# Low parts of the down-projection weights made by accumulating DMA transfers instead of by VectorE

## The chip, the cores and the metric

The kernel runs on one core of a Trainium2 chip. The core has TensorE (matrix products out of SBUF into PSUM), VectorE, ScalarE and GpSimd (POOL) for work by element, SyncE (SP), which here only issues transfers, and 16 DMA engines. Each engine takes its instructions in the order of its own queue and waits on semaphores for the others. The metric is the device time of one execution in microseconds. Times inside the kernel come from one profiled execution, counted from its first instruction.

## The reference

The reference is a trunk of two encoder layers on 256 positions of width 2048, in float32. Layer 0 mixes tokens by grouped-query attention, layer 1 by a dilated sliding-window attention. Each layer is followed by a gated MLP, which is where the change lies:

```python
D_MODEL = 2048
SEQ = 256
DEPTH = 2
D_FF = 5632
...
def conv_ffn(h, w_up, conv_w, conv_b, w_down):
    u = h @ w_up
    c = u.shape[-1]
    pad = CONV_WIDTH // 2
    u = lax.conv_general_dilated(u, conv_w[:, None, :].astype(u.dtype), window_strides=(1,),
                                 padding=((pad, pad),), dimension_numbers=('NWC', 'WIO', 'NWC'),
                                 feature_group_count=c) + conv_b
    gate, val = jnp.split(u, 2, axis=-1)
    return (jax.nn.silu(gate) * val) @ w_down
...
    for i in range(DEPTH):
        hn = rms_norm(h, mix_norm[i])
        ...
        h = h + conv_ffn(rms_norm(h, ffn_norm[i]), w_up[i], conv_w[i], conv_b[i], w_down[i])
    return rms_norm(h, final_norm)
```

The down-projection multiplies a 256 x 5632 matrix by the 5632 x 2048 weights `w_down`, once in each layer.

## The kernel before

**Precision.** TensorE takes its operands in a float32 format of lower precision (`F32R`). To come near float32, each matrix is split into a high part, which is the value rounded to that format, and a low part, which is the difference. A product is then made of three: high by high, high by low, low by high. For the weights, the high part `wh` is a copy made by ScalarE (line 139) and the low part `wl` a subtraction made by VectorE, `raw - wh` (line 140). For the activations the two parts lie in `ah` and `al` (in `xh` and `xl` elsewhere).

**The unit of work.** `feed` (line 114) handles 512 rows of a weight matrix by 512 columns. SP loads them as one transfer of 1 MB into a tile `raw` of 128 partitions by 4 x 512 values (line 118). The tile is worked on in two halves (`s` = 0 and 1), each of 128 x 1024 values: `wh`, `wl`, then 12 matmuls, which are three products for each of two groups of 128 rows of weights (`kt`) and two groups of 128 positions (`m`). The results add up in two PSUM tiles `accs`. After each half `step()` runs one stage of whatever work is pending, such as the transposition of earlier results.

**Buffers and order.** `raw` has three buffers (`NRAW`), `wh` and `wl` three each (`NHL`). The order of the instructions on each queue is made by a scheduler when the program is built, by priorities that follow the program's text. The work on `wh` and `wl` stands in `tc.high_priority(offset=AHEAD)` with `AHEAD` = 45, so it is placed as if it stood 45 instructions earlier, and it then waits for a free buffer rather than for its turn. A load of `raw` waits for the last reader of the buffer that it takes.

**The stages.** `ffn` (line 291) is called once for each layer. It does the MLP in two parts (`HALVES`), over 6 and then 5 groups of 512 inner columns: the up-projection by `feed_T` (line 90), with the convolution and the gate behind it, whose last product is made by GpSimd (`cv`, line 354), and then the down-projection of that part (lines 431 to 436). The down-projection goes over four column blocks `n`: blocks 0 and 1 together in `project2` (line 158), which leaves the last group of each to a late part, and blocks 2 and 3 by `project` (line 151), one after the other. A part has so 4 x 6 = 24 or 4 x 5 = 20 feeds, 88 in both layers. In the very last block the last feed is run with `by_m`: all matmuls of one group of positions first, so that its results can be finished early. In the second part of layer 1, the results of blocks 0 to 2 are multiplied by the final gain `fin` on GpSimd (line 399).

**Other users of the same code.** `feed` also serves the projections of both attentions, which the change leaves as they are.

Of the kernel before, what the change touches and what calls it, by code (L numbers as in the profile page):

```python
# [7 lines left out]
F32 = mybir.dt.float32  # L8
F32R = mybir.dt.float32r
AF = mybir.ActivationFunctionType  # L10
ALU = mybir.AluOpType
AX = mybir.AxisListType

P = 128
# [9 lines left out]
AHEAD = 45  # L24
# [4 lines left out]
def tile_encoder(ctx: ExitStack, tc: tile.TileContext, x, xT, w_a, w_ao, q_gain, k_gain, w_b, w_bo,  # L29
                 rel_bias, gains, w_up, conv, w_down, final_norm, rope, ident_c, onehot, out):  # L30
    nc = tc.nc
# [24 lines left out]
    def nm(s):  # L56
        uid[0] += 1
        return f"{s}_{uid[0]}"
# [15 lines left out]
    def start(gen):  # L74
        if next(gen, StopIteration) is not StopIteration:
            pending.append(gen)

    def step():
        while pending:
            if next(pending[0], StopIteration) is not StopIteration:  # L80
                return
            pending.pop(0)
        if spare and next(spare[0], StopIteration) is StopIteration:
            spare.pop(0)

    def drain(keep=0):
        while len(pending) > keep:
            step()
# [22 lines left out]
                                 start=False, stop=end and kt == 3)  # L111
            step()

    def feed(accs, lhs, kg, wap, first, last, by_m=False, pieces=1, mid=None):
        raw = spool.tile([P, 4, 512], F32, tag="raw", name=nm("raw"), bufs=NRAW)
        rawf, w = raw.rearrange("p a c -> p (a c)"), 2048 // pieces
        for i in range(pieces):
            nc.sync.dma_start(rawf[:, i * w:(i + 1) * w], wap[:, i * w:(i + 1) * w])
            if mid is not None:
                mid(i)  # L120
        def mms(order):
            for m, kt in order:
                (wh, wl), j = hls[kt // 2], kt % 2
                xh, xl = lhs[4 * kg + kt][:2]
                st, sp = first and kt == 0, last and kt == 3
                c = slice(m * P, (m + 1) * P)
                nc.tensor.matmul(accs[m], xh[:, c], wh[:, j, :], start=st, stop=False)  # L127
                nc.tensor.matmul(accs[m], xh[:, c], wl[:, j, :], start=False, stop=False)  # L128
                nc.tensor.matmul(accs[m], xl[:, c], wh[:, j, :], start=False, stop=sp)  # L129

        hls = []
        for s in range(2):
            wh = spool.tile([P, 2, 512], F32R, tag="wh", name=nm("wh"), bufs=NHL)
            wl = spool.tile([P, 2, 512], F32R, tag="wl", name=nm("wl"), bufs=NHL)
            r = raw[:, 2 * s:2 * s + 2, :]
            with tc.high_priority(offset=AHEAD):
                for i in range(max(pieces // 2, 1)):
                    c = slice(i, i + 1) if pieces == 4 else slice(0, 2)
                    nc.scalar.activation(wh[:, c], r[:, c], AF.Copy)  # L139
                    nc.vector.tensor_tensor(wl[:, c], r[:, c], wh[:, c].bitcast(F32), ALU.subtract)  # L140
            hls.append((wh, wl))
            if not by_m:
                mms([(m, kt) for kt in (2 * s, 2 * s + 1) for m in range(2)])
                step()
        if by_m:
            mms([(m, kt) for m in range(2) for kt in range(4)])

    def new_acc():
        return [accp.tile([P, 512], F32, tag="acc", name=nm("acc")) for _ in range(2)]

    def project(w, n, lhs, kgs, by_m=False):
        accs = new_acc()
        for i, kg in enumerate(kgs):
            end = i == len(kgs) - 1
            feed(accs, lhs, kg, w[n, kg], i == 0, end, by_m and end)
        return accs

    def project2(w, n0, n1, lhs, kgs, late, first_done, hook=None):
        a0, a1 = new_acc(), new_acc()
        early = len(kgs) - late  # L160
        for k, part in enumerate((range(early), range(early, len(kgs)))):
            if k == 1:
                drain()
            for accs, n in ((a0, n0), (a1, n1)):
                for i in part:
                    kg = kgs[i]
                    mid = hook and hook(n == n0, kg)
                    feed(accs, lhs, kg, w[n, kg], i == 0, i == len(kgs) - 1,
                         pieces=4 if hook and i < 2 else 2 if hook else 1, mid=mid)
                if k == 1 and n == n0:  # L170
                    first_done(a0)
        return a1
# [39 lines left out]
    def sumsq_cols(ss, n, junk):  # L212
        for m in range(2):
            nc.scalar.activation(junk(), h[:, m, n * 512:(n + 1) * 512], AF.Square,
                                 accum_out=ss[:, m, n:n + 1])
# [54 lines left out]
    def add_residual(accs, n):  # L270
        for m in range(2):
            hs = h[:, m, n * 512:(n + 1) * 512]
            nc.vector.tensor_tensor(hs, accs[m], hs, ALU.add)  # L273
# [17 lines left out]
    def ffn(l, hT, ss_in, g_next, last, side=None):  # L291
        with tc.tile_pool(name=nm("fpool"), bufs=1) as fp:
# [66 lines left out]
            kgs = list(range(4))  # L359
            for hf, (p0, p1) in enumerate(HALVES):  # L360
                slots = {}
# [29 lines left out]
                def done(accs, n):  # L391
                    if hf == 1 and last:
                        for m in range(2):
                            cols = slice(n * 512, (n + 1) * 512)
                            hs = h[:, m, cols]
                            nc.vector.tensor_tensor(hs, accs[m], hs, ALU.add)
                            if n < 3:
                                nc.scalar.activation(junk(), hs, AF.Square, accum_out=ss[:, m, n:n + 1])
                                nc.gpsimd.tensor_tensor(hs, hs, fin[:, cols], ALU.mult)
                            else:  # L400
                                nc.vector.scalar_tensor_tensor(junk(), hs, 1.0, hs, ALU.mult, ALU.mult,
                                                               accum_out=ss[:, m, n:n + 1])
                                finish(m)
                        if n == 2:
                            nc.vector.tensor_reduce(part, ss[:, :, :3], axis=AX.X, op=ALU.add)
                            nc.vector.tensor_scalar(part, part, 1.0 / D, EPS, op0=ALU.mult, op1=ALU.add)
                        return
                    add_residual(accs, n)
                    if hf == 1:
                        sumsq_cols(ss, n, junk)  # L410
                        start(late_transpose(hTn, n, g_next, fp, "tT"))

                def finish(m):
                    ms = small.tile([P, 1], F32, tag="ms", name=nm("ms"))
                    nc.vector.tensor_scalar(ms, ss[:, m, 3:4], 1.0 / D, part[:, m:m + 1],
                                            op0=ALU.mult, op1=ALU.add)
                    r = small.tile([P, 1], F32, tag="rstd", name=nm("rstd"))
                    nc.gpsimd.tensor_tensor(r, ms, nhalf[:, :1], ALU.pow)
                    for n in (3, 0, 1, 2):
                        hs = h[:, m, n * 512:(n + 1) * 512]  # L420
                        if n == 3:
                            nc.vector.scalar_tensor_tensor(hs, hs, r, fin[:, n * 512:(n + 1) * 512],
                                                           ALU.mult, ALU.mult)
                        elif n == 0 or m == 0:
                            nc.scalar.activation(hs, hs, AF.Copy, scale=r)
                        else:
                            nc.vector.tensor_scalar(hs, hs, r, None, op0=ALU.mult)
                        eng = nc.scalar if m == 1 and n % 2 == 0 else nc.sync
                        eng.dma_start(out.rearrange("(p m) c -> m p c", m=2)[m, :, n * 512:(n + 1) * 512], hs)

                np_ = p1 - p0
                drain(1)
                wd = w_down[l][:, p0:p1]
                done(project2(wd, 0, 1, slots, list(range(np_)), 1, lambda a: done(a, 0)), 1)
                for n in (2, 3):
                    done(project(wd, n, slots, list(range(np_)), last and hf == 1 and n == 3), n)
            assert not spare
        return hTn, ss

# [49 lines left out]
    def mixer_a():  # L489
        with tc.tile_pool(name="apool", bufs=1) as ap:  # L490
# [95 lines left out]
            def k_gen(accs):  # L586
# [9 lines left out]
                yield from heads_T_dve(kT, ro, ap, "sq")  # L596

            va = project2(w_a, 4, 5, hT, kgs, 1, lambda a: start(k_gen(a)), hook)
            v = evac_split(ap, va, rstd[0])

# [56 lines left out]
            for g in range(4):  # L657
                start(attend(g, project(w_a, g, hT, kgs)))
# [249 lines left out]
```

## Time and profile before

| | |
|---|---|
| time, median of 2 runs | 2312.73 us (2312.73 to 2312.74) |
| span of the profiled execution | 2312.0 us |
| mean granted TensorE clock | 0.999 |
| down-projection stages (first to last load of `w_down`) | 529 to 656, 883 to 991, 1823 to 1950, 2177 to 2283 us |
| loads of `w_down` | 88 of 1024 KB |
| data moved by DMA | 437.46 MB, mean 189 GB/s |

The page gives for each engine its busy time, its share of the span and its number of instructions; PEld are the weight loads of TensorE, which run beside its matmuls. In the rows of instructions, the first number of a timeline row is its start and the second its duration, in microseconds, and what stands in square brackets is the idle time ahead of it on its engine and who ended it. A row of waits gives the sum of the waits, their number and the longest. A row of a transfer ends with its size and the time from its issue to its landing. In a table of stretches, the last three columns are the granted TensorE clock, the busy share of the DMA engines and the rate that they moved. A matmul row lasts longer than the distance to the next one, since matmuls are pipelined: the distance is the cost.

### The profile page before, as it was taken

What the parts mean: (1) busy time and instruction counts of PE and PEld (TensorE: products, weight loads), DVE (VectorE), ACT (ScalarE), POOL (GpSimd) and SP (SyncE); (2) the same over time, 40 slices, a digit from 0 to 9 for tenths busy, and PEclk for the clock granted to TensorE, in tenths of its full rate; (3) what the DMA queues carried; (4) which work ended last, traced back from release to release, by engine and by line L of the source; (5) the groups of instructions that cost most, each with busy time, mean ns of one, the idle gap of its engine ahead of it and who ended that gap; (6) DMA issues with size and microseconds to landing.
All of it is one profiled execution on the core that took longest, in us unless ns stands there. A gap on an engine that the chain in (4) does not pass through costs nothing.

```text
span 2312.0 us, 30191 instructions
## 1 busy us (share of the span) xinstructions
PE 2292.1 (99%) x11641; PEld 1946.0 (84%) x11641; DVE 1613.9 (70%) x2321; ACT 1210.7 (52%) x1746; POOL 162.4 (7%) x127
## 2 busy tenths in 40 slices
PE   9999999999999999999999999999999999999998
PEld 7788788888888888888888888878888888888886
DVE  6877877676457776778776876586777754677755
ACT  6565565554345555455454554445555543555543
POOL 2210000010000010010000000000101100001010
PEclk9999999999999999999999999999999999999999
DMA  8444565665555555565555554556555555555554
GB/s 289 156 146 148 190 201 180 229 201 194 187 195 191 191 184 189 181 222 200 195 178 174 174 198 164 172 190 212 186 191 190 191 186 198 191 191 183 193 190 146
DMA packets 229024, 437.46 MB, mean 189 GB/s; under 512 B 10400, under 2 KB 193440, under 8 KB 201104
## 3 DMA queue, kind: packets, MB, share of 16 engines
q1 hardware_dynamic: 226976, 429.82, 55.2%
q0 software_dynamic: 1472, 5.15, 0.7%
q8 instruction: 91, 1.49, 0.3%
q10 hardware_dynamic: 432, 0.56, 0.1%
q14 instruction: 53, 0.43, 0.0%
HBM read 429.20 MB, written 6.29 MB: 188 GB/s over the span
## 4 chain that ended last, share of the span: by engine, by line
PE 89%; DVE 6%; DMA 2%; issue 1%; POOL 1%; ACT 1%; SPq 1%; POOLq 0%; DVEq 0%; ACTq 0%
PE acc L107 26%; PE acc L128 15%; PE acc L129 15%; PE acc L127 15%; PE acc L110 14%; DVE wl L140 2%; DVE tT L219 2%; DMA raw<-in_w_up_dram 2%; PE ps L190 1%; PE ps L194 1%; PE ps L193 0%; PE ps L192 0%; POOL t L576 0%; SPq L685 0%; DVE h L273 0%
## 5 line engine op out<-in xcount | busy, mean ns | idle before, releaser
L140 DVE TENSOR_TENSOR wl<-raw,wh 128x1024 fp32r<-128x1024 f32 (+1 forms) x456 | 552.6, 1214 | 333.1 <-ACT wh L139 329.5
L139 ACT ACTIVATE wh<-raw 128x1024 fp32r<-128x1024 f32 (+1 forms) x456 | 475.1, 1044 | 545.6 <-PE acc L129 494.5
L107 PE MATMUL acc<-xh,wh 128*128 128x512 f32 x2816 | 707.5, 393 | 3.1 <-ACT wh L102 3.0
L107 PEld LDWEIGHTS acc<-xh,wh 128*128 128x128 f32 x2816 | 507.1, 189 | 95.7 <-ACT wh L102 4.1
L103 DVE TENSOR_TENSOR wl<-raw,wh 128x1024 fp32r<-128x1024 f32 x352 | 431.7, 1228 | 202.1 <-ACT wh L102 191.7
L102 ACT ACTIVATE wh<-raw 128x1024 fp32r<-128x1024 f32 x352 | 372.1, 1058 | 311.1 <-PE acc L107 204.4
L110 PEld LDWEIGHTS acc<-xh,wl 128*128 128x128 f32 x2816 | 384.1, 190 | 27.5
L128 PE MATMUL acc<-wl,ah 128*128 128x512 f32 x1024 | 400.1, 391 | 2.5 <-DVE wl L140 2.2
L127 PE MATMUL acc<-wh,ah 128*128 128x512 f32 x1024 | 399.2, 390 | 0.0
L129 PE MATMUL acc<-wh,al 128*128 128x512 f32 x1024 | 398.8, 389 | 0.0
L110 PE MATMUL acc<-xh,wl 128*128 128x256 f32 x2816 | 392.6, 282 | 0.0
L127 PE MATMUL acc<-wh,xh 128*128 128x512 f32 x768 | 302.3, 394 | 0.9 <-ACT wh L139 0.9
L128 PE MATMUL acc<-wl,xh 128*128 128x512 f32 x768 | 300.3, 391 | 2.2 <-DVE wl L140 2.1
L129 PE MATMUL acc<-wh,xh 128*128 128x512 f32 x768 | 299.6, 390 | 0.0
L128 PEld LDWEIGHTS acc<-wl,ah 128*128 128x128 f32 x1024 | 192.3, 188 | 46.5 <-DVE wl L140 7.6
L127 PEld LDWEIGHTS acc<-wh,ah 128*128 128x128 f32 x1024 | 192.3, 188 | 39.7
L129 PEld LDWEIGHTS acc<-wh,al 128*128 128x128 f32 x1024 | 192.3, 188 | 39.4
L354 POOL TENSOR_TENSOR cv<-cg,cv 128x512 f32<-128x512 f32 x44 | 95.5, 2170 | 1165.4 <-DVE cv L346 975.4
L128 PEld LDWEIGHTS acc<-wl,xh 128*128 128x128 f32 x768 | 144.4, 188 | 32.6 <-DVE wl L140 5.3
L129 PEld LDWEIGHTS acc<-wh,xh 128*128 128x128 f32 x768 | 144.2, 188 | 29.9
L127 PEld LDWEIGHTS acc<-wh,xh 128*128 128x128 f32 x768 | 144.4, 188 | 29.4 <-ACT wh L139 1.7
L178 ACT ACTIVATE ah<-cv 128x256 fp32r<-128x256 f32 x88 | 32.0, 411 | 105.1 <-POOL cv L354 105.1
(152 smaller groups left out, 1374.8 us busy)
## 6 DMA issues: line engine op xcount, KB each, us to landing
raw<-in_w_up_dram SPq DMA_DIRECT2D x352, 512.0 KB
raw<-in_w_down_dram SPq DMA_DIRECT2D x88, 1024.0 KB
raw<-in_w_b_dram SPq DMA_DIRECT2D x72, 1024.0 KB
raw<-in_w_bo_dram SPq DMA_DIRECT2D x24, 1024.0 KB
raw<-in_w_a_dram SPq DMA_DIRECT2D x16, 1024.0 KB
raw<-in_w_ao_dram SPq DMA_DIRECT2D x16, 1024.0 KB
raw<-in_w_a_dram SPq DMA_DIRECT2D x16, 256.0 KB
raw<-in_w_a_dram SPq DMA_DIRECT2D x8, 512.0 KB
```

Source lines behind the costliest of these rows:

```text
L102: nc.scalar.activation(wh, rk, AF.Copy)
L103: nc.vector.tensor_tensor(wl, rk, wh.bitcast(F32), ALU.subtract)
L107: nc.tensor.matmul(acc[j], wh[:, kt, j * P:(j + 1) * P], lhs[4 * kg + kt][2], start=first and i == 0 and kt == 0, stop=False)
L110: nc.tensor.matmul(acc[j][:, :NT], wl[:, kt, j * P:(j + 1) * P], lhs[4 * kg + kt][0], start=False, stop=end and kt == 3)
L127: nc.tensor.matmul(accs[m], xh[:, c], wh[:, j, :], start=st, stop=False)
L128: nc.tensor.matmul(accs[m], xh[:, c], wl[:, j, :], start=False, stop=False)
L129: nc.tensor.matmul(accs[m], xl[:, c], wh[:, j, :], start=False, stop=sp)
L139: nc.scalar.activation(wh[:, c], r[:, c], AF.Copy)
L140: nc.vector.tensor_tensor(wl[:, c], r[:, c], wh[:, c].bitcast(F32), ALU.subtract)
L178: nc.scalar.activation(hi, src, AF.Copy)
L219: nc.vector.transpose(o[cols].rearrange("p a (m t) -> p a m t", m=2)[:, :, :, rows], s[rows].rearrange("p m (a c) -> p a m c", c=P)[:, :, ...
L354: nc.gpsimd.tensor_tensor(cv, cg, cv, ALU.mult)
```

## The change

In the down-projections, the second half of each feed gets its low part in another way. ScalarE makes `wh` as before, and then a second copy, `-wh`, into a tile `wd` (two buffers, in the pool of `ffn`). GpSimd issues a transfer that adds the raw weights onto it, so that `wd` holds `raw - wh`. In layer 0 this transfer reads the weights from DRAM a second time, in layer 1 it reads them from the tile `raw`. The matmuls of that half are reordered: first the eight that use `wh`, then the four that use the low part. The first half of each feed, the feed run with `by_m`, and the projections of the attentions stay as they are.

```diff
-    def feed(accs, lhs, kg, wap, first, last, by_m=False, pieces=1, mid=None):
+    def feed(accs, lhs, kg, wap, first, last, by_m=False, pieces=1, mid=None, low=None):
...
-        def mms(order):
+        def mms(order, late_low=False):
             for m, kt in order:
                 (wh, wl), j = hls[kt // 2], kt % 2
                 xh, xl = lhs[4 * kg + kt][:2]
                 st, sp = first and kt == 0, last and kt == 3
                 c = slice(m * P, (m + 1) * P)
                 nc.tensor.matmul(accs[m], xh[:, c], wh[:, j, :], start=st, stop=False)
-                nc.tensor.matmul(accs[m], xh[:, c], wl[:, j, :], start=False, stop=False)
-                nc.tensor.matmul(accs[m], xl[:, c], wh[:, j, :], start=False, stop=sp)
+                if not late_low:
+                    nc.tensor.matmul(accs[m], xh[:, c], wl[:, j, :], start=False, stop=False)
+                nc.tensor.matmul(accs[m], xl[:, c], wh[:, j, :], start=False, stop=sp and not late_low)
+            if late_low:
+                for m, kt in sorted(order) if last else order:
+                    nc.tensor.matmul(accs[m], lhs[4 * kg + kt][0][:, m * P:(m + 1) * P],
+                                     hls[kt // 2][1][:, kt % 2, :], start=False, stop=last and kt == 3)
...
         for s in range(2):
             wh = spool.tile([P, 2, 512], F32R, tag="wh", name=nm("wh"), bufs=NHL)
+            r = raw[:, 2 * s:2 * s + 2, :]
+            by_dma = low is not None and s == 1
+            if by_dma:
+                pool, from_dram = low
+                wl = pool.tile([P, 2, 512], F32R, tag="wd", name=nm("wd"), bufs=2)
+                with tc.high_priority(offset=AHEAD):
+                    nc.scalar.activation(wh, r, AF.Copy)
+                    nc.scalar.activation(wl, wh.bitcast(F32), AF.Copy, scale=-1.0)
+                    src = wap[:, 1024:2048].rearrange("p (a c) -> p a c", c=512) if from_dram else r
+                    nc.gpsimd.dma_start(wl, src, accum_op=ALU.add)
+                hls.append((wh, wl))
+                mms([(m, kt) for kt in (2, 3) for m in range(2)], True)
+                step()
+                continue
             wl = spool.tile([P, 2, 512], F32R, tag="wl", name=nm("wl"), bufs=NHL)
-            r = raw[:, 2 * s:2 * s + 2, :]
...
                 wd = w_down[l][:, p0:p1]
-                done(project2(wd, 0, 1, slots, list(range(np_)), 1, lambda a: done(a, 0)), 1)
+                low = (fp, l == 0)
+                done(project2(wd, 0, 1, slots, list(range(np_)), 1, lambda a: done(a, 0), low=low), 1)
                 for n in (2, 3):
-                    done(project(wd, n, slots, list(range(np_)), last and hf == 1 and n == 3), n)
+                    done(project(wd, n, slots, list(range(np_)), last and hf == 1 and n == 3, low), n)
```

`project` and `project2` pass `low` on to `feed`; `project` leaves it out for the feed that is run with `by_m`.

More of the change, by code (lines that the diff above doesn't have):

```diff
@@ L149, in new_acc, with project @@
         return [accp.tile([P, 512], F32, tag="acc", name=nm("acc")) for _ in range(2)]
-    def project(w, n, lhs, kgs, by_m=False):
+    def project(w, n, lhs, kgs, by_m=False, low=None):
         accs = new_acc()
@@ L154, in project, with project2 @@
             end = i == len(kgs) - 1
-            feed(accs, lhs, kg, w[n, kg], i == 0, end, by_m and end)
+            feed(accs, lhs, kg, w[n, kg], i == 0, end, by_m and end, low=None if by_m and end else low)
         return accs
-    def project2(w, n0, n1, lhs, kgs, late, first_done, hook=None):
+    def project2(w, n0, n1, lhs, kgs, late, first_done, hook=None, low=None):
         a0, a1 = new_acc(), new_acc()
@@ L168, in project2 @@
                     feed(accs, lhs, kg, w[n, kg], i == 0, i == len(kgs) - 1,
-                         pieces=4 if hook and i < 2 else 2 if hook else 1, mid=mid)
+                         pieces=4 if hook and i < 2 else 2 if hook else 1, mid=mid, low=low)
                 if k == 1 and n == n0:
```

## The prediction, made before the result was known

> **What bounds the kernel now.** I read the page first, then the stages in which the changed lines run, then one stretch of the timeline there, then the rows of the transfers.
>
> ```profile
> span 2312.0 us, 30191 instructions
> ...
> PE 2292.1 (99%) x11641; PEld 1946.0 (84%) x11641; DVE 1613.9 (70%) x2321; ACT 1210.7 (52%) x1746; POOL 162.4 (7%) x127
> ...
> PE 89%; DVE 6%; DMA 2%; issue 1%; POOL 1%; ACT 1%; SPq 1%; POOLq 0%; DVEq 0%; ACTq 0%
> ```
>
> TensorE is busy for 99% of the span, and 89% of the chain of waits is its own work. VectorE, which the change relieves, is 70% busy. Its share of the chain is 6%, but that is an average over attention and projections. The table of stretches shows the four down-projection stages alone:
>
> ```profile
> core 0: us, PE busy (x) PEld busy (x) DVE busy (x) ACT busy (x) POOL busy (x), PEclk, DMA share, GB/s
> 529.00:656.00 127.00, 127.00 (x588) 106.19 (x587) 68.58 (x74) 54.14 (x60) 4.41 (x2) 1.00 0.56 191
> 883.00:991.00 108.00, 107.49 (x499) 89.40 (x498) 78.50 (x114) 53.58 (x72) 4.40 (x2) 1.00 0.54 185
> 1823.00:1950.00 127.00, 127.00 (x587) 106.18 (x587) 68.37 (x73) 54.30 (x60) 4.40 (x2) 1.00 0.56 191
> 2177.00:2283.00 106.00, 106.00 (x495) 88.81 (x494) 62.26 (x68) 50.52 (x64) 13.57 (x8) 1.00 0.55 189
> ```
>
> In 468 us of these stages TensorE is idle for about 0.5 us, at full granted clock. VectorE works 54 to 73% of them. So there is hardly anything to win where the change acts. What waits of TensorE on `wl` exist in the whole program are these:
>
> ```profile
> PE acc L128 <- DVE wl L140: 4.3, 10, 0.9
> PEld acc L128 <- DVE wl L140: 12.9, 20, 1.3
> ```
>
> The matmul row, 4.3 us, is the most that a faster `wl` gives back; the 12.9 us are of the weight loads, which run ahead of the matmuls. The question is only whether the new way of making `wl` is ready in time. For that I read the timeline in layer 0:
>
> ```profile
> 560.02 0.39 PE L129 MATMUL acc<-wh,al 128*128 128x512 f32 x1
> ...
> 560.25 0.39 PE L127 MATMUL acc<-wh,ah 128*128 128x512 f32 x1
> ...
> 560.45 1.06 ACT L139 ACTIVATE wh<-raw 128x1024 fp32r<-128x1024 f32 x1 [1.61 <-PE acc L129]
> ...
> 561.54 1.23 DVE L140 TENSOR_TENSOR wl<-raw,wh 128x1024 fp32r<-128x1024 f32 x1 [1.45 <-ACT wh L139]
> ...
> 562.79 22.09 SPq L118 DMA_DIRECT2D raw<-in_w_down_dram  x5
> ...
> 562.97 0.39 PE L127 MATMUL acc<-wh,ah 128*128 128x512 f32 x1
> 563.17 1.06 ACT L139 ACTIVATE wh<-raw 128x1024 fp32r<-128x1024 f32 x1 [1.66 <-PE acc L129]
> ...
> 565.69 0.39 PE L127 MATMUL acc<-wh,ah 128*128 128x512 f32 x1
> ```
>
> The matmuls come in blocks of 12, one block for each half of a `feed`: they start at 560.25, 562.97 and 565.69, so a block takes 2.72 us, a matmul 2.72/12 = 0.227 us, and a feed of two blocks 5.44 us. The load of the next `raw` leaves at 562.79, as the `wl` of 561.54 ends (561.54 + 1.23 = 562.77): this `wl` was the last reader of its `raw`, so it belongs to the second half of a feed, the half that is changed. `wh` has three buffers. ScalarE waited for the block that ended just before 560.45; the two other buffers serve the blocks of 560.25 and 562.97, so the buffer written at 560.45 serves the one of 565.69.
>
> **The change part by part.** *Removed from VectorE:* the second-half subtraction of 87 feeds (88, less the last one, which is run by rows), 87 x 1.23 = 107 us. It was off the path: ready at 562.77 for a block at 565.69. The gain is between 0 and the 4.3 us above; I take 0.
>
> *Added on ScalarE:* 87 negated copies. No row shows one; the nearest is the rounding copy of the same shape, 1.06 us, so 87 x 1.06 = 92 us. In the stretch above ScalarE idles 1.66 us before each `wh`, so one copy fits into one of two such gaps per feed: no cost of its own. Without that cover it would delay every `wh`, which itself has 565.69 - 561.51 = 4.2 us in hand.
>
> *Matmuls:* the same 24 a feed; in a changed half the four low ones come last. That moves their need to 565.69 + 8 x 0.227 = 567.51. They wait for a transfer now, and everything behind them on TensorE waits with them, though its own operands are there.
>
> *Added on POOL:* 87 issues of an accumulating transfer. What the rows have of transfers issued there, and of the loads beside which they must run:
>
> ```profile
> q1 hardware_dynamic: 226976, 429.82, 55.2%
> ...
> fin<-in_final_norm_dram POOLq DMA_DIRECT2D x1, 1024.0 KB, 5.1
> ...
> oh<-in_onehot_dram POOLq DMA_DIRECT2D x1, 512.0 KB, 3.9
> ```
>
> ```profile
> 1572.00:1581.00 9.00, 9.00 (x58) 8.10 (x57) 6.18 (x10) 5.60 (x10) 2.72 (x7) 1.00 0.85 284
> ```
>
> ```profile
> 274.94 0.56 POOL L667 DMA_DIRECT2D oh<-in_onehot_dram  x1
> ...
> 2245.37 2.97 POOL L399 TENSOR_TENSOR h<-h,fin 128x512 f32<-128x512 f32 x2 [41.75 <-ACT junk L398]
> ```
>
> The clock of a changed half: `wh` from 560.45 to 561.51, the negation to 562.57, issue at 562.6, need at 567.51. So issue to landing may take **4.9 us** before TensorE stands still. If it takes L, the feed takes 5.44 + (L - 4.9) us: the issue hangs on the end of the previous feed's first block, which moves with the stall, so the lateness is paid again in every feed and not caught up.
>
> How long is L? A plain 512 KB landed in 3.9 us and a plain 1024 KB in 5.1, the latter with the engines at 0.85. That is 1.2 us per 512 KB on top of 2.7. An accumulating transfer must bring in what lies at its destination as well as its source. Lower bound: it costs as a plain one, 3.9, hidden. Upper bound: three passes (two reads, one write) at the rate of the loads, 429.82 MB in 0.552 x 2312 us = 337 GB/s, or 1.56 us per 512 KB, and a whole raw load (3.1 us) in front: 2.7 + 4.7 + 3.1 = 10.5 us. I take two operands, which is fin's 5.1, and 0.8 us more for the raw load that starts at almost the same moment: half of one 1.56 us pass, between nothing (fin already ran beside loads) and a full pass. For this load's release moves as well: in layer 0 it leaves when `wh` of the second half is done (561.5, about 1.1 us before the accumulation), and in layer 1, where the accumulation reads `raw`, when that has landed, L after its issue; the next issue follows a feed, L + 0.5 us, after the last one, so the load leaves 0.5 us ahead of it. Whether the source is DRAM (44 feeds of layer 0) or `raw` (43 of layer 1), the same bytes pass the engines. L = 5.9, a feed 6.44 us, 87 x 1.0 = **+87 us**.
>
> The Trainium skill speaks against the change here. Its page "Collectives: The Full Stack" (The bandwidth ceiling: the fold count and why AG ≠ RS ≠ AR) says that an addition in the DMA engines needs two source reads per chunk where a copy needs one, and that this about halves the rate. No run here shows that so far; by it the 512 KB cost as the 1024 KB of fin.
>
> *The engines' capacity* is no second bill at two operands but close: 3.1 us of raw load and 2 x 1.56 of accumulation are 6.2 us in a feed of 6.44. With the feed at 5.44 they would not fit, so 87 x 0.8 = 70 us is owed even if latency were free, provided both reads cost in full.
>
> *POOL's own queue:* issuing takes 0.56 us, 87 x 0.56 = 49 us in an idle engine. Behind a waiting issue stand the last gate products of the up stage (needed some 50 us later, by the late part of `project2`), and ahead of some issues in the last stage stand six products with `fin`, of some 1.5 us each in pairs (2.97): an issue behind a pair is late by up to 3 us. Three pairs at 1.5 us on average add 4.5 us.
>
> *Raw in layer 1* is kept until the landing instead of 562.77. At L = 5.9 the load then leaves at 562.6 + 5.9 = 568.5 for a `wh` two feeds after the one of 563.17, at 563.17 + 2 x 6.44 = 576.05: 7.5 us, in which a load of 3.1 us with 2.7 us of start fits. I cost it at nothing; if that cover is gone, it adds some tenths of a microsecond in 43 feeds, under 20 us.
>
> Sum against the profiled execution: 2312.0 + 87 + 4.5 = 2403.5. The median of the runs, 2312.73, lies 0.7 above the span, so **2404 us**.
>
> **The rivals.**
>
> *Hidden (not slower).* If L stays at or below 4.9 us, all of it hides under the two blocks ahead, and the result is 2312.7, less at most 4.3: 2308 to 2313. The decision lies at 4.9 us; a loss of 2%, 46 us, needs 46/87 = 0.53 more, L = 5.4. For it: oh's 3.9, and even fin's 5.1 would cost only 0.2 x 87 = 17 us, 2330 us. Against it: neither adds anything on the way, and both were single transfers, not one per 5.4 us. In a sentence apart: the Trainium skill, "DMA: Bandwidth & Descriptors" (Anatomy of one DMA — SWDGE (gpsimd) path), gives 2.0 us plus the bytes at 436 GB/s, an estimated 3.2 us for 512 KB, by which this rival would hold; both rows here are 0.7 us above that formula.
>
> *The adding itself is slow.* If the engines' adders or the read-then-write of each row cost four or five passes instead of two, L is 2.7 + 4 x 1.2 = 7.5 up to 8.7, a feed 8.0 to 9.2, and the loss 226 to 331 us: 2539 to 2644. Nothing in the trace shows an addition in a transfer, for or against.
>
> *Raw becomes late in layer 1 only.* Then layer 1's stages grow and layer 0's don't; with L at 5.9 it is the 20 us above, 2424.
>
> **How the numbers follow.** Forecast with its neighbours, L from 5.45 to 7.4, that is 2361 to 2535, and raw's lateness with it: 0.47. Hidden or nearly (L below 5.4): 0.36, of which most lies between 2308 and 2359. Slow adding, above 2535: 0.15. Something faster than 2266 has no mechanism in stages where TensorE never waits: 0.02. The range for 8 in 10 takes in the hidden case and half of the slow one: 2308 to 2600; the likeliest case alone is 2361 to 2535. The 2% (46 us) are about what a measurement of this kernel can tell from no change. Faster 0.02; same 0.36; slower 0.62.
>
> **What would show it.** In the changed profile: POOL issues of `wd` x87 with their time to landing (forecast 5.9, decision at 4.9); an idle of TensorE before the low matmuls, released by a DMA, of about 1 us in each changed half; raw loads in the down stages 6.4 us apart instead of 5.44; stretches of 529 and 1823 that grow from 127 to about 151 us; VectorE 107 us lighter, ScalarE 92 us heavier. The forecast is wrong if the landing takes under 5 us, if the raw loads and not the accumulations are what is waited for, or if the up stages, which are not changed, take part in the loss.

## The result, and the profile after

The changed kernel takes **2457.11 us** (median of 2 runs, 2455.42 to 2458.81) against 2312.73: a ratio of 1.062, interval 1.059 to 1.066, slower by 144 us. The profiled execution has a span of 2453.6 us, 141.6 above the one of before.

The page of the changed kernel: busy times, the chain of waits, and the transfers issued on POOL with their sizes and times to landing.

```profile
span 2453.6 us, 30517 instructions
...
PE 2343.2 (95%) x11641; PEld 1966.3 (80%) x11641; DVE 1507.5 (61%) x2234; ACT 1294.5 (53%) x1833; POOL 237.5 (10%) x214
...
PE 75%; DMA 13%; issue 5%; DVE 4%; ACT 2%; POOL 1%; POOLq 0%; SPq 0%; DVEq 0%; ACTq 0%
...
wd<-in_w_down_dram POOLq DMA_DIRECT2D x44, 512.0 KB, 7.2
wd<-raw POOLq DMA_DIRECT2D x43, 512.0 KB, 5.2
```

VectorE lost 106 us of work, ScalarE gained 84, and DMA, which had 2% of the chain, now has 13%. The median landing is 7.2 us where the weights come from DRAM (layer 0) and 5.2 us where they come from `raw` (layer 1). TensorE waits for it, as the rows of waits of the low matmuls of the changed halves (line 133) show:

```profile
PE acc L133 <- DMA wd<-in_w_down_dram: 49.9, 36, 2.8
PE acc L133 <- DMA wd<-raw: 41.5, 20, 3.4
```

That is 91.4 us in 56 pauses.

The down stages in the table of stretches:

```profile
core 0: us, PE busy (x) PEld busy (x) DVE busy (x) ACT busy (x) POOL busy (x), PEclk, DMA share, GB/s
531.00:694.00 163.00, 140.91 (x604) 111.37 (x602) 44.34 (x53) 76.16 (x83) 22.81 (x23) 0.97 0.85 222
923.00:1060.00 137.00, 118.86 (x512) 94.39 (x510) 64.15 (x107) 71.66 (x93) 19.20 (x19) 0.96 0.83 219
1894.00:2061.00 167.00, 145.87 (x615) 116.52 (x614) 46.48 (x56) 78.60 (x85) 23.23 (x24) 0.94 0.80 217
2289.00:2440.00 151.00, 134.08 (x565) 107.79 (x565) 44.77 (x56) 74.21 (x88) 30.86 (x27) 0.93 0.75 206
```

Two things changed there. TensorE is idle for 17 to 22 us in each stage. And the granted clock, 1.00 before, is 0.93 to 0.97. Where it goes is seen in short stretches around one pause of 1.93 us in layer 1:

```profile
1929.00:1931.00 2.00, 0.07 (x2) 0.01 (x1) 0.58 (x1) 1.38 (x2) 0.85 (x1) 1.00 0.58 113
1931.00:1933.00 2.00, 2.00 (x7) 1.57 (x8) 0.64 (x1) 0.00 (x0) 0.00 (x0) 0.73 1.04 197
1933.00:1935.00 2.00, 2.00 (x6) 1.61 (x5) 0.00 (x0) 0.00 (x0) 0.00 (x0) 0.50 1.01 229
1935.00:1937.00 2.00, 2.00 (x9) 1.62 (x9) 0.00 (x0) 0.44 (x1) 0.00 (x0) 0.92 1.07 414
```

```profile
1930.99 1.32 PE L133 MATMUL acc<-wd,ah 128*128 128x512 f32 x4 [1.93 <-DMA wd<-raw]
1932.11 0.63 PE L127 MATMUL acc<-wh,ah 128*128 128x512 f32 x1
1932.54 0.63 PE L129 MATMUL acc<-wl,ah 128*128 128x512 f32 x1
...
1935.68 0.39 PE L127 MATMUL acc<-wh,ah 128*128 128x512 f32 x1
1935.91 0.39 PE L129 MATMUL acc<-wl,ah 128*128 128x512 f32 x1
```

After the pause the matmuls follow each other every 0.43 us (1932.11 to 1932.54) instead of 0.23 (1935.68 to 1935.91): TensorE runs at half clock for some 3.4 us (by the three clocks, (0.27 x 2 + 0.50 x 2 + 0.08 x 2)/0.5). Half of that, 1.7 us, is lost, nearly the length of the pause once more.

Together: 91.4 us of waits for landings; from the granted clock at most 0.03 x 163 + 0.04 x 137 + 0.06 x 167 + 0.07 x 151 = 31 us (at most, since part of the half clock can fall on idle time); 56 pauses that each also expose the end of a matmul (0.39 us long, 0.23 apart), 56 x 0.16 = 9 us; and 4 us for the new order of the matmuls (first experiment). That is 135 of the 141.6 us; the rest isn't assigned.

### The profile page after: what moved, and what is told of

Its sections match the earlier page's. It is cut to its first block, busy times and chain, and to the rows that moved or that the text cites. A ratio compares the mean times of both kernels' runs of the same rounds, so it can differ in the third digit from the quotient of the medians.

```text
span 2453.6 us, 30517 instructions
## 1 busy us (share of the span) xinstructions
PE 2343.2 (95%) x11641; PEld 1966.3 (80%) x11641; DVE 1507.5 (61%) x2234; ACT 1294.5 (53%) x1833; POOL 237.5 (10%) x214
## 3 DMA queue, kind: packets, MB, share of 16 engines
q0 software_dynamic: 14000, 50.77, 10.9%
## 4 chain that ended last, share of the span: by engine, by line
PE 75%; DMA 13%; issue 5%; DVE 4%; ACT 2%; POOL 1%; POOLq 0%; SPq 0%; DVEq 0%; ACTq 0%
PE acc L107 25%; PE acc L110 13%; PE acc L127 10%; PE acc L130 10%; PE acc L129 10%; DMA wd<-in_w_down_dram 7%; DMA wd<-raw 5%; PE acc L133 3%; DVE wl L158 2%; DVE tT L237 2%; DMA raw<-in_w_up_dram 1%; ACT wd L146 1%; ACT wh L145 1%; PE ps L208 1%; PE ps L212 0%
## 5 line engine op out<-in xcount | busy, mean ns | idle before, releaser
L158 DVE TENSOR_TENSOR wl<-raw,wh 128x1024 fp32r<-128x1024 f32 (+1 forms) x369 | 443.4, 1204 | 495.6 <-ACT wh L157 492.7
L157 ACT ACTIVATE wh<-raw 128x1024 fp32r<-128x1024 f32 (+1 forms) x369 | 381.6, 1037 | 312.2 <-PE acc L130 266.9
L102 ACT ACTIVATE wh<-raw 128x1024 fp32r<-128x1024 f32 x352 | 372.2, 1058 | 322.1 <-PE acc L107 216.4
L127 PE MATMUL acc<-wh,ah 128*128 128x512 f32 x1024 | 408.7, 399 | 0.0
L130 PE MATMUL acc<-wh,al 128*128 128x512 f32 x1024 | 406.3, 397 | 0.0
L129 PE MATMUL acc<-wl,ah 128*128 128x512 f32 x676 | 272.7, 403 | 2.0 <-DVE wl L158 1.8
L145 ACT ACTIVATE wh<-raw 128x1024 fp32r<-128x1024 f32 x87 | 92.3, 1061 | 281.7 <-PE acc L130 277.4
L127 PEld LDWEIGHTS acc<-wh,ah 128*128 128x128 f32 x1024 | 198.3, 194 | 43.0
L133 PE MATMUL acc<-wd,ah 128*128 128x512 f32 x348 | 110.9, 444 | 91.4 <-DMA wd<-in_w_down_dram 49.9
L130 PEld LDWEIGHTS acc<-wh,xh 128*128 128x128 f32 x768 | 144.3, 188 | 30.0
L133 PEld LDWEIGHTS acc<-wd,ah 128*128 128x128 f32 x348 | 65.1, 203 | 127.9 <-DMA wd<-in_w_down_dram 65.9
```

The lines of the kernel that those rows point to most:

```text
L102: nc.scalar.activation(wh, rk, AF.Copy)
L133: nc.tensor.matmul(accs[m], lhs[4 * kg + kt][0][:, m * P:(m + 1) * P], hls[kt // 2][1][:, kt % 2, :], start=False, stop=last and kt == 3)
L145: nc.scalar.activation(wh, r, AF.Copy)
```

## The experiments

Theory A: TensorE waits for accumulating transfers that land too late; all else is cover. Its rivals: the added copies and the order of the matmuls cost; the DMA engines' capacity is the bound; in layer 1 the kept `raw` tile is. Experiments 4 and 5 were run four times each, the others once.

**1. No transfer, all the rest.**

```diff
-                    nc.gpsimd.dma_start(wl, src, accum_op=ALU.add)
+                    nc.vector.tensor_tensor(wl, r, wl.bitcast(F32), ALU.add)
```

> Everything of the change stays (negated copy on ScalarE, the low matmuls last) except the transfer: VectorE adds raw onto the negated copy. Theory A, late landing: TensorE waits for the transfers alone, so the time returns to that of before, 2308 to 2320 us, with no half-clock spells in the down stages. Rival, the added ScalarE copies or the new order of the matmuls cost: some 10 us or more above before, spread over all down stages.

Measured: 2318.95 us, beside 2313.51 for the kernel before on the same chip. TensorE's waits on the low parts of these halves fall to 1.0 us, so the transfer makes the loss. What is left, 5 us, shows in the distance from one changed half to the next in the timeline:

```profile
576.50 1.06 ACT L145 ACTIVATE wh<-raw 128x1024 fp32r<-128x1024 f32 x1 [2.38 <-PE acc L130]
...
581.99 1.06 ACT L145 ACTIVATE wh<-raw 128x1024 fp32r<-128x1024 f32 x1 [2.39 <-PE acc L130]
```

A feed takes 5.49 us here and 5.44 before: 0.05 us, or 87 x 0.05 = 4.4 us in all. TensorE has no idle time in these feeds, so the matmuls themselves are a little farther apart. Most likely that is their new order; the copies and the order were not tested apart.

**2. A transfer that only copies.**

```diff
-                    nc.gpsimd.dma_start(wl, src, accum_op=ALU.add)
+                    nc.gpsimd.dma_start(wl, src)
```

> The transfer only copies the raw half onto wd and does not add (so the low parts of these halves are left out of the result, and raw takes their place). Same issue, same bytes moved to the same place. If the adding is what makes the landing late, it falls from 7.2 and 5.2 us to 3.9 to 5.0 and the time to 2313 to 2340 us. If a transfer of 512 KB beside a raw load takes that long anyway, the landing stays at 6 to 7 us in layer 0 and the time above 2400 us.

Measured: 2367.17 us, between the two cases. The copies land after 5.4 us out of DRAM and 3.9 out of SBUF, where the accumulations took 7.2 and 5.2. So 1.8 and 1.3 us of the landing go with the adding. The issue on POOL, too, takes 0.54 us instead of 0.87 (medians 540 and 872 ns). But a plain copy is already late in this place: adding is not all of it.

**3. The same transfers, with nobody waiting for them.**

```diff
-                    nc.gpsimd.dma_start(wl, src, accum_op=ALU.add)
+                    nc.vector.tensor_tensor(wl, r, wl.bitcast(F32), ALU.add)
+                    dump = pool.tile([P, 2, 512], F32R, tag="dump", name=nm("dump"), bufs=2)
+                    nc.scalar.activation(dump, wh.bitcast(F32), AF.Copy, scale=-1.0)
+                    nc.gpsimd.dma_start(dump, src, accum_op=ALU.add)
```

> The low part is made by VectorE as in the run before it; beside that the same accumulating transfers run onto a tile that nobody reads. Theory A: TensorE waits for nothing new, 2310 to 2325 us, though the transfers land as late as in the change. Rival B, the transfers take so much of the DMA engines, or keep raw so long, that the raw loads are late: 2370 us or more, with ScalarE waiting for raw.

Measured: 2351.19 us, and the layers differ. In the timeline of SP, the first stages of the two layers from their first to their last load of `w_down` (before: 126.94 us each):

```profile
527.68 129.05 SPq L118 DMA_DIRECT2D raw<-in_w_down_dram  x24
...
1825.34 149.68 SPq L118 DMA_DIRECT2D raw<-in_w_down_dram  x24
```

In layer 0 the stage is as long as in the first experiment (129.05 there too), though the transfers land after 9.1 us: theory A. From the first load of `w_down` in layer 0 to the first in layer 1 it takes 1825.34 - 527.68 = 1297.7 us, where the first experiment takes 1297.2. So the engines carry these transfers at the old pace, if only just: from 545 to 680 us their share is 1.01, and TensorE is busy all the time. In layer 1 the stage is 21 us longer than in the first experiment, and ScalarE waits for raw loads:

```profile
ACT wh L160 <- DMA raw<-in_w_down_dram: 70.9, 32, 6.1
```

There a slow transfer, even one that nobody waits for, keeps its `raw` tile, and the next load comes late: the rival holds for this layer.

**4. An earlier start.**

```diff
-            wh = spool.tile([P, 2, 512], F32R, tag="wh", name=nm("wh"), bufs=NHL)
             by_dma = low is not None and s == 1
+            if by_dma:
+                wh = low[0].tile([P, 2, 512], F32R, tag="wz", name=nm("wh"), bufs=2)
+            else:
+                wh = spool.tile([P, 2, 512], F32R, tag="wh", name=nm("wh"), bufs=NHL)
...
-                wl = pool.tile([P, 2, 512], F32R, tag="wd", name=nm("wd"), bufs=2)
+                wl = pool.tile([P, 2, 512], F32R, tag="wd", name=nm("wd"), bufs=3)
```

> The change, with buffers of its own for the rounded part of the second half (two) and three instead of two for wd, so that the chain rounding, negating, adding can start up to a feed earlier. Theory A: with 4.9 plus at least 2.7 us in hand the landings of 5 to 7 us are mostly hidden; 2312 to 2335 us. Rival B, engine capacity: two operands want 6.2 us of the engines in a feed of 5.44, so the feed cannot be shorter than about 6 us, 2360 us or more, whatever is in hand.

Measured: 2432.39 us, ratio 1.050 (1.046 to 1.054). That is in rival B's range, but not for its reason: the time is lost in layer 1, where the share of the DMA engines is 0.76 (stretch of 1845 to 2040), while layer 0, at 0.95 (531 to 660), comes near to theory A. The first stages again, and then one run of layer 1:

```profile
529.20 128.62 SPq L118 DMA_DIRECT2D raw<-in_w_down_dram  x24
...
1843.26 191.62 SPq L118 DMA_DIRECT2D raw<-in_w_down_dram  x24
```

```profile
1908.27 0.85 POOL L151 DMA_DIRECT2D wd<-raw  x1 [8.22 <-ACT wd L149]
1908.40 1.46 PE L133 MATMUL acc<-wd,ah 128*128 128x512 f32 x4 [1.87 <-DMA wd<-raw]
1908.48 18.44 SPq L118 DMA_DIRECT2D raw<-in_w_down_dram  x3
...
1917.29 0.86 POOL L151 DMA_DIRECT2D wd<-raw  x1 [8.17 <-ACT wd L149]
1917.40 1.20 PE L133 MATMUL acc<-wd,ah 128*128 128x512 f32 x4 [1.59 <-DMA wd<-raw]
```

Layer 0's stage falls from 157.85 us in the change to 128.62: with more in hand most of the lateness is hidden. The loads run further ahead of the matmuls here, so the distance from the first load of `w_down` in layer 0 to the first in layer 1 is the safer measure: 1293.8 us before, 1363.9 in the change, 1314.1 here. Of 70 us, 50 are won back, and TensorE still waits 11.1 us for landings in this layer. In layer 1 the stage grows from 164.26 to 191.62. The issue of 1908.27 has landed by 1917.40, a full feed of 9.0 us later. Only when a landing lets go of `raw` does a raw load leave (1908.48, just after the wait that ended at 1908.40). ScalarE waits for a raw load until 1914.99, and the next negated copy comes behind that on ScalarE (1915.95), so that the next issue leaves at 1917.29. The earlier start turned this into a chain that runs in step. Why the landings themselves take 9 us here, where 4.5 is the least, was not tested.

**5. The earlier start, both layers out of DRAM.** As 4, with `low = (fp, True)`.

> As the run with more buffers, but layer 1 reads its weights again from DRAM too, so raw is free as soon as it has been rounded and need not wait for the landing. Theory A1: in layer 1 it was the held raw tile that made feeds of 9 us; now layer 1 behaves as layer 0 did there (20 us over before), so about 2313 + 2 x 20 = 2353 us, 2335 to 2365. Rival: layer 1 has another obstacle (its POOL products, its order), and the time stays above 2400.

Measured: 2356.44 us, ratio 1.018 (1.016 to 1.020), as expected. The held `raw` tile was what layer 1 had against it, and most of the loss of the change can be bought back with 12 KB of buffers in each partition and the second reading of the weights. It doesn't beat the kernel before. The landings have grown to 8.3 us, the engines are nearly full (a share of 0.94 from 531 to 667 us), and TensorE still waits 23.0 us for landings.

**6. The change, both layers out of DRAM.** `low = (fp, True)` alone.

> The change with its own buffers, both layers from DRAM. Layer 0 of the change lost 72 us with landings of 7.2; layer 1 should now show the same landings (6.3 to 8.9 instead of 4.5 to 9.4), feeds of 6.6 us without the pattern of three, and about the same loss: 2313 + 2 x 72 = 2457, 2440 to 2470 us. If reading from raw was what cost layer 1 its time, it gets clearly better: under 2430.

Measured: 2435.54 us in one run, under the expected range, 22 us less than the change. The landings, 7.1 us in the median, and the feeds, (149.33 - 0.33)/23 = 6.5 us between the loads of layer 1's first stage, are as expected or nearly, but layer 1 gained more. The waits don't tell why; the granted clock does:

```profile
PE acc L133 <- DMA wd<-in_w_down_dram: 91.2, 77, 2.7
```

```profile
core 0: 2433.7 us, clock 0.996
```

TensorE waits 91.2 us for landings, as long as in the change (91.4). But it is 77 pauses of at most 2.7 us instead of 56 of up to 3.4, and the mean granted clock of the execution is 0.996 instead of 0.983. TensorE's busy time is 18.8 us shorter (2324.4 against 2343.2), which is nearly all of the 19.9 us between the two profiled executions. Long, rare pauses cost more here than short, frequent ones of the same sum.

**7. Idle work in the pause.**

```diff
             if late_low:
+                fill = ps_tile()
+                for _ in range(4):
+                    nc.tensor.matmul(fill, lhs[4 * kg + 2][0][:, :P], hls[1][0][:, 0, :], start=True, stop=True)
```

> The change with four more matmuls in each changed half, ahead of the low ones, whose result nobody reads: 87 x 4 x 0.227 = 79 us of added TensorE work, in the place where it stands idle. If the pauses cost more than their length because TensorE goes to half clock after them, the half-clock spells go and the time falls below that of the change: 2415 to 2440 us. If the clock costs nothing, added work can only leave the time as it is or raise it: 2457 us or more.

Measured: 2450.05 us in one run, above the expected 2415 to 2440 and yet 7 us below the change, with 79 us more work; the granted clock rises to 0.996. Waits on landings fall to 37.3 us. Lower time with more work speaks for the clock; but 7 us are little, in one run, and the fillers cost time where a landing was early. The busy time says more: with 79 us of fillers it grows by 48 us only (2343.2 to 2391.1). The other 31 us are about what the clock was put at above.

**8. Half the raw loads.**

```diff
+        if low is not None:
+            nc.sync.dma_start(rawf[:, :1024], wap[:, :1024])
-        for i in range(pieces):
+        for i in range(pieces if low is None else 0):
...
-            r = raw[:, 2 * s:2 * s + 2, :]
+            r = raw[:, 0:2, :] if low is not None else raw[:, 2 * s:2 * s + 2, :]
```

> The change with only the first half of each raw tile loaded in the changed down-projections, and both halves made from it (the second half of those weights is left out of the result). The loads beside the accumulating transfers fall from 1024 to 512 KB a feed. If the landing is late because the transfer shares the engines with the raw load, it falls from 7.2 to 5.0 to 5.8 us in layer 0 and the time to 2320 to 2370 us. If an accumulation onto SBUF out of DRAM takes 7 us by itself, it stays at 6.5 or more and layer 0 keeps its loss.

Measured: 2415.99 us. Layer 0's landing falls from 7.2 to 6.7 us only, so the second case holds: sharing with the raw load is a small part (0.5 us for half of it), and an accumulation of 512 KB out of DRAM takes most of its 7 us with half the loads beside it, too. The time is 41 us below the change all the same: TensorE waits 74.1 us instead of 91.4, and the granted clock is 0.995 instead of 0.983.

## Why the prediction was right

The forecast was slower, 2404 us, and the mechanism a landing that comes after the low matmuls need it. That is what happened; the forecast was 53 us short. Its 87 us of pauses meet the measured 91.4, but that is luck: their length and their price were both off, as told below. (The 46 us that the prediction takes for the least that can be told are far too many: the runs of the kernel before lie between 2312.5 and 2315.7 us.)

- *Nothing to win.* VectorE lost the 106 us and TensorE gained nothing: its matmuls' waits on `wl` were 4.3 us before and are 3.9 after.
- *ScalarE's copies are covered.* Right: in the first experiment ScalarE has them all, and only 5 us are lost. The order of the matmuls, to which they most likely belong, was costed at nothing; it would be 0.05 us a feed.
- *The landing, L = 5.9 us.* Mis-sized for layer 0: 7.2. Two operands were priced as twice the bytes, fin's 5.1 us, plus 0.8 for the raw load. The raw load's part was about right (0.5 us for half of it, experiment 8), but a plain copy in this place already takes 5.4 us, not oh's 3.9, and the adding another 1.8. The POOL issue alone grows by 0.33 us. For layer 1 the median of 5.2 hides a pattern: three landings in a row of, for example, 4.5, 7.4 and 4.8 us. It has the rhythm of the three `raw` buffers; that they cause it was not shown.
- *"The lateness is paid again in every feed and not caught up."* Half wrong, and in the other direction. Between the block that frees a `wh` buffer and the low matmuls that need the result lie two pauses, the previous feed's and the own one, and both give the transfer time. So a landing that is x late costs x/2 a feed. With 0.29 us from the end of the copy to the issue, which was set at 0.03, layer 0 should then pause (7.2 + 0.3 - 4.9)/2 = 1.3 us a feed and take 5.49 + 1.3 = 6.8. Measured are (157.85 - 0.33)/23 = 6.85 between loads, in experiment 6 (153.60 - 0.33)/23 = 6.66 with 7.1 us, in experiment 2 (137.40 - 0.33)/23 = 5.96 with 5.4 us, where the formula gives 5.9. By the rule as it was put, 7.2 us would have made 7.7. The two errors, L too small and its price too high, partly cancelled: the feed was forecast at 6.44. Layer 1 doesn't follow the formula: its median of 5.2 us would give 5.8, and its feeds measure (164.26 - 0.33)/23 = 7.13, since the pauses go by the long landings and the half clock comes on top.
- *The clock.* Missing from the sum: up to 31 us, most of them in layer 1. The pauses were costed at their length.
- *POOL's own queue, 4.5 us.* Not seen: the three pairs of products with `fin` in the last stage end 0.8 to 1.7 us before the issue behind them, which waits for its negated copy (the pair of 2370.15 to 2373.44, then the issue of 2374.26).
- *Raw in layer 1, "under 20 us".* The bound holds, though the sum has it at nothing: from its first load of `w_down` to the end, layer 1 takes 559.2 us in the change and 545.2 with its weights out of DRAM (experiment 6), 14 us less. But it comes by the long pauses and the clock, not by ScalarE waiting for raw (7.0 us), and it becomes the bound once the start is moved ahead (experiment 4).
- *Capacity, "70 us is owed even if latency were free".* Too high, in layer 0 at least. Its 44 feeds would owe 44 x 0.8 = 35 us; with the same transfers and nobody waiting for them the layer loses 0.5 us against the first experiment (experiment 3). The 43 us that are left with both layers out of DRAM and more in hand (experiment 5) are an upper bound for both layers, since TensorE still waits for landings there.
- *The Trainium skill's two pages.* By the fixed-plus-bytes formula of the Trainium skill, "DMA: Bandwidth & Descriptors" (Anatomy of one DMA — SWDGE (gpsimd) path), estimated at 3.2 us for 512 KB, the transfer would have been hidden; plain copies of 512 KB took 3.9 and 5.4 us here, so the measurement decides against it in this place. The two source reads of an addition in the Trainium skill, "Collectives: The Full Stack" (The bandwidth ceiling: the fold count and why AG ≠ RS ≠ AR), fit the direction. The share of the queue with these transfers shows the size:

```profile
q0 software_dynamic: 14000, 50.77, 10.9%
```

With the same packets and bytes this share is 6.5% of a span of 2365.4 us in experiment 2 and 10.9% of 2453.6 here: 154 against 267 us of the engines, 1.7 times as much for adding as for copying.

## What to carry to other kernels

Moving work off an engine that nobody waits for gains next to nothing, and it costs where the new way lands later than the buffers in front of it allow: count the time from the moment when a buffer comes free to the need, and compare it with a landing measured in that traffic. A transfer that reads a shared staging tile also keeps that tile, and can delay the loads behind it. And a short pause of TensorE may cost more than its length, so look at the granted clock beside the waits.

## What the runs showed of the hardware

- A pause of TensorE of 1.93 us was followed by some 3.4 us at half clock. At the same sum of waits (91 us), 56 pauses of up to 3.4 us left a mean granted clock of 0.983 (the change), 77 pauses of up to 2.7 us one of 0.996 (experiment 6). At 74 us, 39 pauses of up to 3.5 us left 0.986 (experiment 4), 58 of up to 3.1 us 0.995 (experiment 8).
- An accumulating transfer of 512 KB issued on POOL took 0.85 to 0.87 us to issue and 7.2 us in the median to land out of DRAM, 5.2 out of SBUF (at the least 4.5), beside raw loads; a plain one 0.54 us, 5.4 and 3.9 (at the least 2.9).
